# Counts and transposes moved, and a store cut in four, in a two-block transformer with three expert stages

## The chip, the cores and the metric

The kernel runs as one launch on one core of a Trainium2 chip. The engines of a core work through queues of their own: TensorE (PE, matmuls, with PEld for its weight loads), VectorE (DVE), ScalarE (ACT), GpSimd (POOL) and SyncE (SP, which here only issues transfers). The metric is the device time of one execution in microseconds; lower is better.

## The reference, cut to what matters

512 tokens of width 1024 go through two blocks, in float32.

```python
# block 1
y   = sigmoid(gate_dn) * (gated_delta_rule(q, k, v, g, beta) @ w_dn_out) \
    + sigmoid(gate_sgu) * (spatial_gating(uv) @ w_sgu_out)
h   = layer_norm(ALPHA * x + y @ w_out)
x   = layer_norm(ALPHA * h + hierarchical_moe(h))          # experts, first stage
# block 2, twice: mixer is fox attention, then mla attention
mod = silu(c) @ w_ada[i] + b_ada[i]                         # shifts, scales, gates
x   = x + g1 * mixer(rmsnorm(x) * (1 + sc1) + sh1)
x   = x + g2 * hier_moe(rmsnorm(x) * (1 + sc2) + sh2)       # experts, second and third stage
```

`hierarchical_moe` picks for each token one of 4 groups and in it 2 of 4 experts, and sums the two experts' outputs `(silu(t @ w_gate) * (t @ w_up)) @ w_down` with their weights; an expert's inner width is 256. The delta rule needs, for each of 8 heads and 8 chunks of 64 tokens, the inverse of a unit lower triangular matrix:

```python
a_mat = where(strict, (k_beta @ k.T) * decay, 0) + eye(64)
u, w  = solve(a_mat, v_beta), solve(a_mat, k_beta * exp(g_cum))
```

## The kernel before, in words

The code is one class. Most weights come as 1 MB tiles `st` on SyncE's queue (L276) and are split into a high and a low part, `wh` by ScalarE (L227) and `wl` by GpSimd or VectorE (L222); a product is then three matmuls, `x,wh`, `xl,wh` and `x,wl` (L389, L390, L391). Each engine issues in program order as the tile scheduler left it, and a tile's buffer must come free before the next tile of its ring is written. SyncE's queue is in order too: it carries the weight tiles, the stores of `ysgu` (L634) and the loads `ast` of the modulation matrix `w_ada` (L1614, three buffers), of which VectorE adds one at a time (L1626, L1628). Those additions are woven into the whole of block 1, one at each weight.

**Mixer of block 1.** `inverse(N)` is a generator. It turns 32x32 blocks of all 64 matrices at once (`T`), solves for the blocks' inverses `W` on VectorE (L907, L909) and yields; then `sgu_out` runs, eight tiles of products whose results VectorE combines with `L633` and SyncE stores (L634) from a ring of three "sy" tiles; then the generator goes on: it clears `X` and `Y` (L913, L914, 128x4096 each, GpSimd) and writes the blocks and their transposes into the diagonals (L917, L918, eight transposes on VectorE). `X` is the buffer that held the low part of sgu's gated input, so it comes free with the last sgu product. `join` then builds the 128x128 inverses from the blocks in eight steps: three cleared "q" tiles (L926) take blocks of `N` in turn (L936, GpSimd), TensorE multiplies them with X (L938) and with Y (L941, L942), ScalarE moves the product between (L940), VectorE subtracts the results from X and Y (L945). Projections for the heads are woven between the steps. The scan over chunks follows.

**Output projection of block 1.** After each of four token tiles `after(t)` normalises the rows, copies them in two pieces to `hp` on ScalarE (L507) and stores these to `hd` in DRAM on ScalarE's queue (L509). ScalarE also copies transposed tiles `xT` for the router's logits (L100), which TensorE reads (L109).

**Expert stages** (`moe`, three times). `route` turns logits into one-hot choices, positions and the row numbers of each expert's tokens (`rows`, L1195). GpSimd then fetches the rows of experts 0, 1 and 2 from `hd` with indirect transfers into `xe` (L1199). The first expert is done from unsplit weights: its rows are transposed on TensorE (`first_in`, L1223), and the gate product runs as L1236. The later experts' rows are transposed and split by `expert_in` (L1211, with `xeh` on ScalarE and `xel` on VectorE) and multiplied by L389 to L391. `behind(a, b)` makes instructions issue after the named ones. `between` is a hook that `expert_up` calls inside an expert to put the previous expert's transposes there.

## Time and profile before

| | us |
|---|---|
| three runs | 2038.22, 2036.07, 2028.91 |
| their median | 2036.07 |
| the profiled execution | 2028.85 |
| its span, first to last instruction | 2027.1 |
| TensorE busy in it | 1799.7 (89%) |

The profiled execution is one of its own, near the fastest of the runs. All rows below are from it, and times in them count from the start of its span. The mean granted TensorE clock over the span was 0.949 of full speed. In a timeline row `x3` after the shapes means that three like instructions stand in one row with their common length, and what follows in brackets is the engine's idle time before them with what ended it.

### The profile page before, as it was taken

The page shows a single profiled execution, that of the slowest core. Times are in us where ns is not written, and L with a number is a line of the kernel's source. Part 1 is how long each engine was busy: PE and PEld are TensorE (multiplying, and loading weights), DVE is VectorE, ACT ScalarE, POOL GpSimd, SP SyncE. Part 2 cuts the span into 40 slices and gives each one's busy share as a digit, 9 for nine tenths or more (in the row PEclk, how much of TensorE's full clock was granted, in tenths as well). Part 3 has the DMA queues.
Part 4 walks back from the last instruction along what each step waited for, and adds up shares of the span by engine and source line. Part 5 has one row for each costly group of instructions (what it writes and reads, how often), then busy time and mean ns, then how long its engine had stood idle before and what let it go on. Part 6 is the DMA issues. An engine that isn't in the chain of part 4 may idle for free. (4 is left out here: it accounts for less than half of the span.)

```text
span 2027.1 us, 30666 instructions
## 1 busy us (share of the span) xinstructions
PE 1799.7 (89%) x11690; PEld 1539.8 (76%) x11690; DVE 1437.6 (71%) x2580; ACT 905.8 (45%) x1706; POOL 522.8 (26%) x402
## 2 busy tenths in 40 slices
PE   6989988798989975999689999959997899996998
PEld 5778766677768775888578998958886777795886
DVE  2786885767875466677857566567988778656997
ACT  3334311223333223687334546326654366633663
POOL 5332335223334421221410001231214100242221
PEclk9999999899989987999899999979998899997999
DMA  8653455353546563798504111539973410336994
GB/s 235 190 174 118 155 175 199 99 171 104 146 124 209 200 256 121 284 360 322 173 21 125 43 64 53 219 130 338 366 285 103 127 44 22 105 156 242 364 373 173
DMA packets 174731, 363.35 MB, mean 179 GB/s; under 512 B 23086, under 2 KB 114814, under 8 KB 162288
## 3 DMA queue, kind: packets, MB, share of 16 engines
q1 hardware_dynamic: 154544, 317.94, 46.4%
q0 software_dynamic: 16528, 32.83, 4.7%
q10 hardware_dynamic: 3504, 10.54, 1.3%
q8 instruction: 94, 1.54, 0.3%
q14 instruction: 61, 0.50, 0.1%
HBM read 337.45 MB, written 47.25 MB: 190 GB/s over the span
## 5 line engine op out<-in xcount | busy, mean ns | idle before, releaser
L227 ACT ACTIVATE wh<-st 128x1024 fp32r<-128x1024 f32 (+2 forms) x331 | 360.2, 1096 | 324.1 <-PE mm L390 86.3
L222 DVE TENSOR_TENSOR wl<-st,wh 128x1024 fp32r<-128x1024 f32 (+3 forms) x250 | 319.8, 1290 | 54.6 <-ACT wh L227 51.3
L222 POOL TENSOR_TENSOR wl<-st,wh 128x1024 fp32r<-128x1024 f32 (+1 forms) x81 | 206.9, 2559 | 295.3 <-ACT wh L227 244.0
L389 PE MATMUL mm<-wh,xeh 128*128 128x256 f32 x720 | 211.4, 294 | 0.0
L390 PE MATMUL mm<-wl,xeh 128*128 128x256 f32 x720 | 204.2, 284 | 0.0
L391 PE MATMUL mm<-wh,xel 128*128 128x256 f32 x720 | 204.0, 283 | 0.0
L389 PE MATMUL mm<-x,wh 128*128 128x512 f32 x448 | 184.4, 412 | 14.8 <-DVE sy L633 12.2
L1628 DVE SCALAR_TENSOR_TENSOR acc<-ast,ca,acc 128x1024 f32<-128x1024 f32 x84 | 146.8, 1747 | 59.9 <-DMA ast<-in_w_ada_dram 58.8
L391 PE MATMUL mm<-x,wl 128*128 128x512 f32 x448 | 183.4, 409 | 0.0
L390 PE MATMUL mm<-x,wh 128*128 128x512 f32 x448 | 182.4, 407 | 0.0
L390 PEld LDWEIGHTS mm<-wl,xeh 128*128 128x128 f32 x720 | 138.6, 192 | 0.2
L389 PEld LDWEIGHTS mm<-wh,xeh 128*128 128x128 f32 x720 | 138.3, 192 | 0.2
L391 PEld LDWEIGHTS mm<-wh,xel 128*128 128x128 f32 x720 | 138.3, 192 | 0.0
L1285 POOL DMA_INDIRECT yd<-ye,rows x42 | 43.0, 1023 | 306.1 <-DVE ye L1282 193.4
L389 PEld LDWEIGHTS mm<-x,wh 128*128 128x128 f32 x448 | 87.2, 195 | 37.8 <-issue 19.1
L389 PE MATMUL mm<-wh,fXH 128*128 128x256 f32 x384 | 112.8, 294 | 0.0
L391 PE MATMUL mm<-wh,fXL 128*128 128x256 f32 x384 | 108.9, 286 | 1.8 <-DVE fXL L222 1.8
L390 PE MATMUL mm<-wl,fXH 128*128 128x256 f32 x384 | 109.9, 286 | 0.0
L390 PEld LDWEIGHTS mm<-x,wh 128*128 128x128 f32 x448 | 87.2, 195 | 17.4 <-issue 1.7
L391 PEld LDWEIGHTS mm<-x,wl 128*128 128x128 f32 x448 | 87.3, 195 | 16.4
L1268 PE MATMUL down<-st,hT 128*128 128x512 f32 x192 | 91.5, 596 | 6.0 <-ACTq L1465 3.9
L1785 DVE TENSOR_REDUCE sst<-s 128x1 f32<-128x512 f32 (+3 forms) x128 | 61.7, 484 | 46.9 <-PE s L1782 46.5
(568 smaller groups left out, 4819.0 us busy)
## 6 DMA issues: line engine op xcount, KB each, us to landing
ast<-in_w_ada_dram SPq DMA_DIRECT2D x96, 512.0 KB
st<-in_w_in_dram SPq DMA_DIRECT2D x32, 1024.0 KB
st<-in_moe_w_gate_dram SPq DMA_DIRECT2D x32, 1024.0 KB
st<-in_moe_w_up_dram SPq DMA_DIRECT2D x32, 1024.0 KB
st<-in_moe_w_down_dram SPq DMA_DIRECT2D x30, 1024.0 KB
st<-in_expert_w_gate_dram SPq DMA_DIRECT2D x16, 1024.0 KB
st<-in_expert_w_up_dram SPq DMA_DIRECT2D x16, 1024.0 KB
st<-in_expert_w_down_dram SPq DMA_DIRECT2D x15, 1024.0 KB
```

Source lines behind the costliest of these rows:

```text
L222: rest = eng.tensor_tensor(l, src, f32(h), op=ALU.subtract)
L227: return self.nc.scalar.activation(out, in_, AF.Copy)
L389: mm(out, lh, rh, start=(start and i == 0), stop=False)
L390: mm(out, lh, rl, start=False, stop=False)
L391: last = mm(out, ll, rh, start=False, stop=(stop and i == n - 1))
L1268: mm(ps[i], whole, st[:, i * 512:(i + 1) * 512], start=True, stop=False)
L1285: return self.nc.gpsimd.indirect_dma_start(out=self.yd[:, :], out_offset=bass.IndirectOffsetOnAxis(ap=dst, axis=0), in_=ye, in_offset=None ...
L1628: nc.vector.scalar_tensor_tensor(acc, st, ca[:, k:k + 1], acc, op0=ALU.mult, op1=ALU.add)
L1785: nc.vector.reduce_max(st, ps[:, :n], axis=AX.X, negate=True)
```

## The change

Four edits.

1. `after(t)`: the normalised rows go to `hd` in four pieces of 256 columns with three buffers, not in two of 512 with one.
2. `inverse`: the eight transposes are made right after the solve, before the yield, into `T` and a new tile `WT`. After the yield VectorE clears X and copies the blocks into it, GpSimd clears Y and ScalarE copies into it. `join` takes its q tiles from the "sy" ring.
3. `route`: token places, counts and the number of extra tokens are issued behind the row numbers; the pair weights behind both the fetches and the row numbers.
4. `moe`: for expert 0 the call of `expert_in` for expert 1, and the fetch behind it, move into `between`, which `expert_up` now calls after the gate product of the unsplit expert.

```diff
@@ -502,11 +502,11 @@
                 logits.finish(t, mv[:, 1:2], mv[:, 0:1])
                 xt = x[:, t, :]
                 self.normalise(xt, xt, mv, gb["ln1_g"], gb["ln1_b"])
-                for i in range(2):
-                    hp = rp.tile([P, 512], F32, tag="hp", name=self.name("hp"), bufs=1)
-                    nc.scalar.activation(hp.rearrange("t (k p) -> t k p", k=KD // 2),
-                                         turned(xt)[:, i * KD // 2:(i + 1) * KD // 2, :], AF.Copy)
-                    nc.scalar.dma_start(self.hd[t * P:(t + 1) * P, i * 512:(i + 1) * 512], hp)
+                for i in range(4):
+                    hp = rp.tile([P, 256], F32, tag="hp", name=self.name("hp"), bufs=3)
+                    nc.scalar.activation(hp.rearrange("t (k p) -> t k p", k=KD // 4),
+                                         turned(xt)[:, i * KD // 4:(i + 1) * KD // 4, :], AF.Copy)
+                    nc.scalar.dma_start(self.hd[t * P:(t + 1) * P, i * 256:(i + 1) * 256], hp)
 
             self.out_proj(x, y, logits, add, after, "e1")
             return x
@@ -856,7 +856,7 @@
             next(inv)
             self.sgu_out(gT)
             X, Y = next(inv)
-            self.t2s(c2, q=3, rt=3)
+            self.t2s(c2, rt=3)
             self.join(N, X, Y)
         with ExitStack() as c2:
             self.t2s(c2, V=3, kd=2, qv1=4)
@@ -907,21 +907,27 @@
                 nc.vector.tensor_tensor(tv, T[:, j + 1:, j:j + 1].to_broadcast([P, n, w]),
                                         W[:, j:j + 1, 0:w].to_broadcast([P, n, w]), op=ALU.mult)
                 nc.vector.tensor_tensor(W[:, j + 1:, 0:w], W[:, j + 1:, 0:w], tv, op=ALU.subtract)
+
+            V = tw.tile([P, 32, 32], F32, name="WT")
+            for j in range(4):
+                sl = slice(32 * j, 32 * j + 32)
+                nc.vector.transpose(T[sl], W[sl].rearrange("p i c -> p c i"))
+                nc.vector.transpose(V[sl], W[sl])
             yield
             X = self.big("X").rearrange("p t d -> p (t d)").rearrange("p (u s) -> p u s", u=32)
             Y = self.b16.tile([P, 32, P], F32, tag="b16", name="Y")
-            nc.gpsimd.memset(X, 0.0)
+            nc.vector.memset(X, 0.0)
             nc.gpsimd.memset(Y, 0.0)
             for j in range(4):
                 sl = slice(32 * j, 32 * j + 32)
-                nc.vector.transpose(across(X[sl, :, sl]), W[sl].rearrange("p i c -> p c i"))
-                nc.vector.transpose(across(Y[sl, :, sl]), W[sl])
+                nc.vector.tensor_copy(X[sl, :, sl], across(T[sl]))
+                self.copy("a", Y[sl, :, sl], across(V[sl]))
         yield X, Y
 
     def join(self, N, X, Y):
 
         nc = self.nc
-        qs = [self.t2("q").rearrange("p (c t) -> p c t", c=4) for _ in range(3)]
+        qs = [self.t2("sy").rearrange("p (c t) -> p c t", c=4) for _ in range(3)]
         for q in qs:
             nc.gpsimd.memset(q, 0.0)
         for u in range(8):
@@ -1121,10 +1127,11 @@
                 nc.tensor.matmul(o, ohp[:, i, k], rb[:, 2 * i + k], start=False, stop=(i + k == NT))
         rows, last = self.rows_of(pool, pi, 16)
         tok = t("tok", [P, LATE, NT])
-        self.places(tok, pi[:, 32 - LATE:32])
-        nc.vector.tensor_copy(cnt, ps[:, 64:80])
-        self.rt = dict(oh=oh, pos=pos, cnt=cnt, tok=tok)
-        self.extra_count(t)
+        with self.behind(last):
+            self.places(tok, pi[:, 32 - LATE:32])
+            nc.vector.tensor_copy(cnt, ps[:, 64:80])
+            self.rt = dict(oh=oh, pos=pos, cnt=cnt, tok=tok)
+            self.extra_count(t)
         return t, rows, ohp, last
 
     def slots_of(self, out, pos):
@@ -1235,6 +1242,8 @@
                 for k in range(KD):
                     nc.tensor.matmul(ps[:, 256 * j:256 * j + 256], xT[:, k, :], st[:, k * 256:(k + 1) * 256],
                                      start=k == 0, stop=k == KD - 1)
+                if j == 0:
+                    between()
                 continue
             for i in range(2):
                 if 2 * j + i == 3:
@@ -1331,7 +1340,7 @@
             with self.behind(last):
                 while sum(not r["raw"] for r, _ in self.ready) < 4:
                     self.prepare()
-            with self.behind(self.hold):
+            with self.behind(self.hold, last):
                 self.route_weights(t, self.lg, ohp)
                 row, after = gate, prepare(self.next, lambda: wk.tile([P, D], F32, tag="ye", name=self.name("tmp"), bufs=2))
                 if gate is not None:
@@ -1345,19 +1354,26 @@
             xT = self.first_in(wk, xe[0])
             self.fetch(src[:, 3:4], xe[0])
             for e in range(17):
-                rest = []
+                rest, coming = [], []
+
+                def tokens():
+                    if e < 15:
+                        coming.append(self.expert_in(wk, xe[(e + 1) % 3]))
+                        if e + 4 < 16:
+                            self.fetch(src[:, e + 4:e + 5], xe[(e + 1) % 3])
 
                 def between():
                     if hid is not None:
                         rest.extend(self.hidden(wk, hid))
+                    else:
+                        tokens()
 
                 if e < 16:
-                    x0 = xT
+                    if e:
+                        tokens()
+                    nxt = self.expert_up(wk, xT, w("g", e), w("u", e), between)
                     if e < 15:
-                        xT = self.expert_in(wk, xe[(e + 1) % 3])
-                        if e + 4 < 16:
-                            self.fetch(src[:, e + 4:e + 5], xe[(e + 1) % 3])
-                    nxt = self.expert_up(wk, x0, w("g", e), w("u", e), between)
+                        xT = coming[0]
                 else:
                     between()
                 if e:
```

What the scheduler makes of it, at three places. Lines of the kernel after are numbered differently: its L1644, L944, L947, L951, L1218, L1230 and L1243 are L1628, L938, L941, L945, L1211, L1223 and L1236 of before.

VectorE behind the solve, from its last step on, in the kernel before (`ast` are modulation loads, `mm` the sgu product that L633 combines):

```order
L909 TENSOR_TENSOR W<-W,tmp 128x31
L1628 SCALAR_TENSOR_TENSOR acc_2468<-ast_2473,ca,acc_2468 128x1024
L1628 SCALAR_TENSOR_TENSOR acc_2468<-ast_2507,ca,acc_2468 128x1024
L1628 SCALAR_TENSOR_TENSOR acc_2468<-ast_2543,ca,acc_2468 128x1024
L1628 SCALAR_TENSOR_TENSOR acc_2468<-ast_2546,ca,acc_2468 128x1024
L1628 SCALAR_TENSOR_TENSOR acc_2468<-ast_2580,ca,acc_2468 128x1024
L633 SCALAR_TENSOR_TENSOR sy_2460<-sy_2460,mm_2509 128x512
L633 SCALAR_TENSOR_TENSOR sy_2500<-sy_2500,mm_2548 128x512
```

and in the kernel after:

```order
L909 TENSOR_TENSOR W<-W,tmp 128x31
L914 STREAM_TRANSPOSE T<-W 32x1024
L915 STREAM_TRANSPOSE WT<-W 32x1024
L914 STREAM_TRANSPOSE T<-W 32x1024
L915 STREAM_TRANSPOSE WT<-W 32x1024
L914 STREAM_TRANSPOSE T<-W 32x1024
L915 STREAM_TRANSPOSE WT<-W 32x1024
L914 STREAM_TRANSPOSE T<-W 32x1024
L915 STREAM_TRANSPOSE WT<-W 32x1024
L1644 SCALAR_TENSOR_TENSOR acc_2477<-ast_2482,ca,acc_2477 128x1024
L1644 SCALAR_TENSOR_TENSOR acc_2477<-ast_2516,ca,acc_2477 128x1024
L633 SCALAR_TENSOR_TENSOR sy_2469<-sy_2469,mm_2518 128x512
```

The eight transposes now stand between the solve and the modulation rows, and the first L633 follows two such rows where it followed five.

VectorE in front of the join and in its first step, before (`qv` are tiles of the woven projections):

```order
L917 STREAM_TRANSPOSE X_2722<-W 32x32x32 x3
L918 STREAM_TRANSPOSE Y<-W 32x32x32 x3
L917 STREAM_TRANSPOSE X_2722<-W 32x32x32
L918 STREAM_TRANSPOSE Y<-W 32x32x32
L727 SCALAR_TENSOR_TENSOR qv_468_3065<-mm_3040,cw,qv_468_3065 128x511
L727 SCALAR_TENSOR_TENSOR qv_475_3107<-mm_3082,cw,qv_475_3107 128x511
L727 SCALAR_TENSOR_TENSOR qv_468_3065<-mm_3040,cw,qv_468_3065 128x510
L727 SCALAR_TENSOR_TENSOR qv_475_3107<-mm_3082,cw,qv_475_3107 128x510
L727 SCALAR_TENSOR_TENSOR qv_468_3065<-mm_3040,cw,qv_468_3065 128x509
L727 SCALAR_TENSOR_TENSOR qv_475_3107<-mm_3082,cw,qv_475_3107 128x509
L945 TENSOR_TENSOR X_2722<-X_2722,sc_2748 128x512
L717 SCALAR_TENSOR_TENSOR qv_468_3065<-th_3070,qv_468_3065 128x512
```

and after:

```order
L919 MEMSET X_2731 128x4096
L633 SCALAR_TENSOR_TENSOR sy_2652<-sy_2652,mm_2704 128x512
L923 COPY X_2731<-T 32x32x32 x4
L1644 SCALAR_TENSOR_TENSOR acc_3039<-ast_3044,ca,acc_3039 128x1024
L727 SCALAR_TENSOR_TENSOR qv_468_3074<-mm_3049,cw,qv_468_3074 128x511
L1644 SCALAR_TENSOR_TENSOR acc_3039<-ast_3047,ca,acc_3039 128x1024
L727 SCALAR_TENSOR_TENSOR qv_468_3074<-mm_3049,cw,qv_468_3074 128x510
L951 TENSOR_TENSOR X_2731<-X_2731,sc_2757 128x512
L727 SCALAR_TENSOR_TENSOR qv_468_3074<-mm_3049,cw,qv_468_3074 128x509
L951 TENSOR_TENSOR Y<-Y,sc_2756 128x512
L1644 SCALAR_TENSOR_TENSOR acc_3039<-ast_3089,ca,acc_3039 128x1024
L963 TENSOR_TENSOR Y<-Y,sc_2775 64x4x64
```

The transposes are gone from here, X is cleared and filled by VectorE with an L633 between, and modulation rows stand among the subtractions of the first steps: five up to the third step's.

TensorE at the first product of the join (the projection `mm` is woven in, each tile 24 matmuls), before:

```order
L391 MATMUL mm_3122<-x_183,wl_3027 128x512
L389 MATMUL mm_3122<-x_192,wh_3026 128x512
L390 MATMUL mm_3122<-x_193,wh_3026 128x512
L391 MATMUL mm_3122<-x_192,wl_3027 128x512
L938 MATMUL sc_2746<-X_2722,q_2738 128x128 x4
L389 MATMUL mm_3122<-x_201,wh_3026 128x512
L390 MATMUL mm_3122<-x_202,wh_3026 128x512
```

and after:

```order
L391 MATMUL mm_3091<-x_147,wl_2689 128x512
L389 MATMUL mm_3091<-x_156,wh_2688 128x512
L390 MATMUL mm_3091<-x_157,wh_2688 128x512
L391 MATMUL mm_3091<-x_156,wl_2689 128x512
L944 MATMUL sc_2755<-X_2731,sy_2747 128x128 x4
L389 MATMUL mm_3091<-x_165,wh_2688 128x512
L390 MATMUL mm_3091<-x_166,wh_2688 128x512
```

Before, 69 matmuls of the projections mm_3040, mm_3082 and mm_3122 stand between the last sgu product and the join's first; after, 33 of mm_3049 and mm_3091.

TensorE at the start of the second expert stage (`gen` takes transposed rows of `xe`, `mm` are expert products), before:

```order
L1223 MATMUL gen_13011<-ident,xe_12853 128x128 x4
L1211 MATMUL gen_13028<-ident,xe_12855 128x128 x4
L1236 MATMUL mm_13045<-st_12130,xeT_13010 128x256 x4
L389 MATMUL mm_13090<-wh_12944,xeh_13026 128x256
L390 MATMUL mm_13090<-wl_12945,xeh_13026 128x256
L1211 MATMUL gen_13073<-ident,xe_12857 128x128 x4
L391 MATMUL mm_13090<-wh_12944,xel_13027 128x256
```

and after:

```order
L1230 MATMUL gen_13044<-ident,xe_12886 128x128 x4
L1243 MATMUL mm_13059<-st_12163,xeT_13043 128x256 x4
L1218 MATMUL gen_13074<-ident,xe_12888 128x128 x4
L389 MATMUL mm_13123<-wh_12977,xeh_13072 128x256
L390 MATMUL mm_13123<-wl_12978,xeh_13072 128x256
L1218 MATMUL gen_13106<-ident,xe_12890 128x128 x4
L391 MATMUL mm_13123<-wh_12977,xel_13073 128x256
```

Half of the first expert's gate product now stands ahead of the second expert's transposes; the split products follow these at once.

## Rows read from the trace of the kernel before

**Rows 1.** The page: busy time, share of the span, instructions.
```profile
PE 1799.7 (89%) x11690; PEld 1539.8 (76%) x11690; DVE 1437.6 (71%) x2580; ACT 905.8 (45%) x1706; POOL 522.8 (26%) x402
```

**Rows 2.** Waits of TensorE over the span: total us, times, longest us.
```profile
PE sc L938 <- POOL q L936: 14.9, 1, 14.9
...
PE gen L1211 <- DMA xe<-hd,rows: 13.5, 3, 6.2
PE mm L389 <- DVE sy L633: 12.2, 2, 7.3
...
PE log L109 <- ACT xT L100: 3.9, 4, 3.0
```

**Rows 3.** Timeline of VectorE: start, length (us), count, idle time before and releaser.
```profile
295.72 0.18 DVE L909 TENSOR_TENSOR W<-W,tmp 128x31 f32<-128x31 f32 x1
...
311.15 1.28 DVE L1628 SCALAR_TENSOR_TENSOR acc<-ast,ca,acc 128x1024 f32<-128x1024 f32 x1 [1.40 <-DMA ast<-in_w_ada_dram]
315.40 3.30 DVE L1628 SCALAR_TENSOR_TENSOR acc<-ast,ca,acc 128x1024 f32<-128x1024 f32 x1 [2.96 <-DMA ast<-in_w_ada_dram]
318.73 1.28 DVE L633 SCALAR_TENSOR_TENSOR sy<-sy,mm 128x512 f32<-128x512 f32 x2
...
347.43 5.71 DVE L1628 SCALAR_TENSOR_TENSOR acc<-ast,ca,acc 128x1024 f32<-128x1024 f32 x2 [7.11 <-DMA ast<-in_w_ada_dram]
```

**Rows 4.** The transposing lines: count, shortest/median/longest ns, first and last start.
```profile
L917 DVE STREAM_TRANSPOSE X<-W x4: 1900/1909/2106, 353.1 to 364.7; 32x1024 f32<-32x1024 f32 x4
...
L918 DVE STREAM_TRANSPOSE Y<-W x4: 1854/1890/1895, 359.0 to 366.6; 32x1024 f32<-32x1024 f32 x4
```

**Rows 5.** Timeline of GpSimd, columns as for VectorE.
```profile
315.27 5.66 POOL L222 TENSOR_TENSOR wl<-st,wh 128x1024 fp32r<-128x1024 f32 x2 [9.25 <-ACT wh L227]
...
339.37 3.52 POOL L913 MEMSET X<- 128x4096 f32 x1 [1.48 <-PE mm L390]
...
368.46 0.99 POOL L926 MEMSET q<- 128x512 f32 x2 [12.59 <-DVE Y L918]
```

**Rows 6.** Stretches: length; PE, PEld, DVE, ACT, POOL busy; clock; DMA share; GB/s.
```profile
340.00:355.00 15.00, 15.00 (x67) 12.22 (x66) 7.85 (x4) 3.73 (x5) 15.00 (x5) 1.00 0.60 208
...
370.00:375.00 5.00, 4.91 (x21) 4.59 (x21) 2.47 (x4) 2.49 (x4) 2.46 (x8) 0.52 0.00 0
```

**Rows 7.** VectorE: a small memset (timeline), copies (group: busy us, mean ns).
```profile
0.83 0.17 DVE L159 MEMSET ones<- 128x128 f32 x1 [0.83 <-PEq L2184]
...
L229 DVE COPY xeT<-gen 128x512 f32<-128x512 f32 x3 | 2.1, 689 | 1.5 <-PE gen L1223 1.5
```

**Rows 8.** Timeline of ScalarE, 748 to 781 us.
```profile
748.77 0.35 ACTq L509 DMA_DIRECT2D hd<-hp  x1
...
756.54 1.14 ACT L507 ACTIVATE hp<-xres 128x512 f32<-128x512 f32 x1 [6.99 <-DMA hd<-hp]
...
779.78 1.21 ACT L507 ACTIVATE hp<-xres 128x512 f32<-128x512 f32 x1 [2.44 <-DMA hd<-hp]
```

**Rows 9.** Timelines of ScalarE, VectorE and GpSimd, 794 to 799 us.
```profile
794.18 0.33 ACTq L509 DMA_DIRECT2D hd<-hp  x1
...
794.84 0.18 DVE L1195 TENSOR_SCALAR rows<-gen 128x32 int32<-128x32 f32 x1
...
797.23 1.26 POOL L1199 DMA_INDIRECT xe<-hd,rows  x1 [13.49 <-DVE tot L1444]
```

**Rows 10.** Timeline of TensorE at the start of the second expert stage.
```profile
1357.09 1.09 PE L1211 MATMUL gen<-ident,xe 128*128 128x128 f32 x4 [6.23 <-DMA xe<-hd,rows]
1357.97 3.53 PE L1236 MATMUL mm<-st,xeT 128*128 128x256 f32 x8
1361.03 0.58 PE L389 MATMUL mm<-wh,xeh 128*128 128x256 f32 x1
```

**Rows 11.** Timelines of ScalarE and VectorE in that stage.
```profile
1358.22 0.60 ACT L227 ACTIVATE xeh<-gen 128x512 fp32r<-128x512 f32 x1 [6.63 <-PE gen L1211]
...
1364.54 1.23 DVE L222 TENSOR_TENSOR wl<-st,wh 128x1024 fp32r<-128x1024 f32 x1 [0.73 <-ACT wh L227]
```

## The prediction

> **What bounds the kernel now.** I read the page first: TensorE is busy 89% of the span [rows 1], so what an edit is worth is the TensorE idle time that it removes. The waits of TensorE come second [rows 2], and the change touches four of them: one of 14.9 us at the first product of the join (L938), one of 7.3 us behind the gated product of the sgu stage (L633), one of 3.0 us behind a transposed tile that ScalarE copies (L100), and 13.5 us in three waits for the second expert's rows (L1211). The timelines of the engines named as releasers come third, because a releaser is only the last link: behind L938 stand eight transposes on VectorE, not GpSimd's small copies.
>
> **The solved blocks: the wait of 7.3 us.** The solve ends at 295.72 + 0.18 = 295.9 [rows 3]. Before, VectorE then took modulation rows (L1628) until 318.7, and freed the bank that TensorE wanted with the first of two L633, at 318.73 + 0.64 = 319.4 [rows 3]. After, the order shows eight transposes, two modulation rows, then that L633. A transpose takes 1.91 or 1.89 us [rows 4], eight 15.2, which ends at 311.1. A modulation row took 1.28 us and in another place 3.30 [rows 3]. So L633 ends between 311.1 + 2.6 + 0.6 = 314.3 and 311.1 + 6.6 + 0.6 = 318.3: a gain of 1.1 to 5.1 us. I take 3.5, nearer the short end, since both loads have then long been issued.
>
> **The wait of 14.9 us.** Before, the X memset began at 339.37, released by TensorE [rows 5], the transposes ran from 353.1 to 366.6 + 1.85 = 368.4 [rows 4], and the q tiles' memsets on GpSimd had stood 12.59 us behind them [rows 5]. After, 3.5 us earlier, TensorE gives X free at about 335.9. Then on VectorE, in series:
> - X memset of 128x4096. GpSimd took 3.52 us for it [rows 5]; VectorE took 0.17 us for 128x128 [rows 7], and 32 of those are 5.4. I take 4.5, the middle.
> - L633, 0.64 us. The memset waits for TensorE at the head of VectorE's queue, and this L633 behind it frees the bank of the projection's second tile: at 341.0, and TensorE comes for it at 335.9 + 24 x 0.224 = 341.3, so it does not wait (0.6 us at the memset's upper bound).
> - four copies of 32x1024. 128x512 took 0.69 us [rows 7], the lower bound; the transposes that write the same strided block took 1.91 [rows 4], the upper. I take 1.0 each, nearer the plain copy.
>
> X is ready at 335.9 + 4.5 + 0.6 + 4.0 = 345.0 (bounds 342.8 and 349.5). TensorE reaches the first join product after 24 + 9 matmuls of the projection; 67 took 15.0 us [rows 6], 0.224 each, so 7.4 us, at 343.3. It waits 1.7 us (0 to 6.2) instead of 14.9 and gains 13.2 (8.7 to 14.9). Before, 69 such matmuls stood ahead of that product; the other 36 now stand behind it and are moved, not saved. The granted clock was 0.52 in the 5 us after the long wait [rows 6], half speed, which costs 2.4 us; without the long idle I take 2.0 of it back (0 to 2.4).
>
> Y costs nothing in this sum: its memset on GpSimd (3.52 us by X's row) and four copies on ScalarE lie beside VectorE's X. ScalarE took 1.14 us for 128x512 with a turned operand [rows 8], so a 32x1024 copy costs 1.1 to 2.3; with 1.5 Y is ready at 335.9 + 3.5 + 6.0 = 345.4, and it is first read about 7 matmuls, 1.6 us, after X. At 2.3 it would be 348.6, some 2 us late. The q tiles now use the "sy" ring, so their memsets wait for ysgu stores, with weight splits (L222) queued behind them on GpSimd. The first waits for the store of the second L633, done by 322; the nearest store took 7 us [rows 8], so 329, and GpSimd has until 335.9 for a memset of 0.5 us [rows 5] and a split. So nothing here either.
>
> **Pieces of hp.** The second piece waited 6.99 us for the store of the first, issued at 748.77, and the copy TensorE needed stood behind it [rows 8]. TensorE had then waited 3.0 us [rows 2]. With four pieces and three buffers, the fourth piece waits for the first store. If that store again takes 7 us, only about 0.5 us is won, since the last piece is half as long; if it comes as soon as in the third token tile, where the wait was 2.44 [rows 8], all 3.0. I take 2.5, since the store is half as large. At the end of this stage rows were ready at 795.0, but the first fetch started at 797.23, about 3 us after the last store was issued at 794.18 [rows 9]: the fetch waits for the store. A fourth piece that is issued about 1 us sooner brings the fetch 1.0 us forward (0 to 1.5).
>
> **Counts behind rows.** Some small VectorE instructions leave the chain to the rows. As the last store ends that chain, not the rows [rows 9], I cost this at 0. Covered so, it stays 0; uncovered, it is a few instructions like the 0.18 us one [rows 9], under 1 us.
>
> **Second expert's transposes.** Before, TensorE waited for the second expert's rows with the first's gate product behind it: 6.2 us in the second stage, and (13.5 - 6.2) / 2 = 3.65 on average in the others [rows 2]. After, part of that product runs in the wait. By the order that is the first half of the gate product, four matmuls that the trace records as eight, 3.53 us [rows 10]. It fits into each wait. What follows the transposes is then limited by their evacuation: the rows land at 1357.09, ScalarE's xeh ends at 1358.22 + 0.60 = 1358.8 [rows 11], and the first split product can start there instead of at 1361.03 [rows 10]: 2.2 us. Some of the following products will run at half clock, as those before them did, so I take 1.5 in each stage (0 to 3.5). In the second stage a copy also moves ahead of a split of 1.23 us [rows 11]; I add 1.0. Together 5.5 (0 to 11). The fetch for expert 4 moves along on GpSimd; its rows are read three experts later.
>
> **Sum.** 3.5 + 13.2 + 2.0 + 2.5 + 1.0 + 5.5 = 27.7 us; all low bounds give 1.1 + 8.7 + 0 + 0.5 + 0 + 0 = 10.3, all high ones 5.1 + 14.9 + 2.4 + 3.0 + 1.5 + 11 = 37.9. The profiled execution took 2028.85 us, so it would take 2001.2. The median of the three runs, 2036.07, lies 7.2 above it, at the upper end of 2028.91 to 2038.22; against the median the sum is 2008.4. I predict 2008, own range 1998 to 2026.
>
> **Rivals.**
> - *The transposes delay L633.* If a modulation load also arrives late, by the 2.96 us of [rows 3], L633 ends at 318.3 + 3.0 = 321.3, 1.9 us later than before instead of 3.5 earlier: 5.4 less, 2014. For it: 15 us of new work ahead of it. Against: five modulation rows stood there before, and two are left. 0.10.
> - *Copies and GpSimd shut each other out.* A modulation row took 3.30 us from 315.40 and 1.28 from 311.15 [rows 3]; GpSimd's splits ran from 315.27 for 5.66 us [rows 5]: 2.0 more beside them. Four copies and the memset, each 2.0 later, make X 10 us later; the stall is 11.7 and the clock falls again: 12 less, 2020. Against: GpSimd's Y memset should be over when the copies start. 0.08. (The Trainium skill, SBUF — State Buffer, section Who interferes with whom, says that an fp32 copy within SBUF takes a pair of ports that VectorE shares with GpSimd, and that whoever comes second is blocked for a whole instruction. The 3.30 us row agrees with such blocking for a two-input instruction; no row shows it for a copy. By that rule this rival, not the sum, would hold.)
> - *The gain is given back.* Join and scan behind it are a chain; if the scan waits for loads that start when they did, the 18.7 us of the first three terms go: 9 left, 2027. Against: loads are issued as buffers come free, so they move along. 0.10.
> - *Not what it says.* Counts behind rows gain nothing, as costed; if the expert stages gain nothing either, since the rows' landing sets their end anyway, 22.2 are left, 2014. For it: cold products. Against: the 2.2 us that L389 started after its operand. 0.04.
> - *Slower.* In the join VectorE's order now puts five modulation rows between the first subtractions that TensorE waits for. The longest wait for such a load was 7.11 us, and two rows behind it took 5.71, 2.85 each [rows 3]. Five times 7.11 + 2.85 is 49.8; less 27.7 that is 22 us slower, 2058. It makes the change a loss from three such waits on, and one above 0.5% from four. For it: the new order. Against: SyncE issues those loads before the join starts. 0.06.
>
> **Chances.** The forecast 0.62. A difference below 0.5%, about 10 us, can't be told from none in this kernel. Faster by more: the forecast, the first two rivals and the fourth, but for 0.02 in their low corner: 0.82; within: the gain given back and that corner, 0.12; slower: 0.06. The range, 1994 to 2027, leaves out half of the given-back case and the slower one; below it reaches 4 us past the own range, since the profiled execution itself lies 7 us under the median.
>
> **What would show it.** Right: the first L633 after the solve ends at 314 to 318 us; the wait of the first join product is under 6 us, with no half clock behind it; no wait of 3 us at L109; the first split product of each expert stage starts within 2 us of the rows' landing. Wrong: a wait of TensorE on X's copies or memset above 6 us, waits in the join on a subtraction that stands behind L1628 on VectorE, or scan waits longer than before.

## The result, and the profile after

The changed kernel takes **2019.57 us** (median of 11 runs, 2009.97 to 2030.86), the kernel before 2036.07 (11 runs beside it, 2027.93 to 2041.52): a ratio of **0.9926, 95% interval 0.9905 to 0.9947**. The forecast was 2008, with a range of 1994 to 2027. The profiled executions stand 2027.1 against 2011.9 us of span, 15.2 us apart, where the sum said 27.7.

The page of the kernel after, the same rows as [rows 1]:

```profile
span 2011.9 us, 30690 instructions
PE 1808.3 (90%) x11690; PEld 1546.0 (77%) x11690; DVE 1439.5 (72%) x2585; ACT 914.4 (45%) x1718; POOL 518.8 (26%) x401
```

To see where the 15.2 us came from, I took the same matmul in both traces at some landmarks, each with as many matmuls ahead of it in both, and subtracted its start after from its start before. A difference between two landmarks is what the stretch between them gained.

| landmark | start before | start after | ahead by | gain of the stretch | the sum had |
|---|---|---|---|---|---|
| ahead of the sgu wait (L391) | 301.39 | 300.90 | 0.49 | | |
| sgu product behind it (L389) | 335.17 | 328.12 | 7.05 | 6.6 | 3.5 |
| behind join and scan (L391) | 607.14 | 599.73 | 7.41 | 0.4 | 15.2 |
| router's product (L109) | 758.54 | 750.27 | 8.27 | 0.9 | 2.5 |
| first expert's first product (L1223, now L1230) | 803.61 | 794.39 | 9.22 | 0.95 | 1.0 |
| second stage, routing (L1099, now L1105) | 1340.52 | 1329.39 | 11.13 | 1.9 | 1.5 |
| third stage, router (L109) | 1822.08 | 1809.02 | 13.06 | 1.9 | 2.5 |
| third stage, a later expert's transposes (L1211, now L1218) | 1865.64 | 1852.47 | 13.17 | 0.1 | 1.5 |

One term of the sum failed: join and scan, 0.4 instead of 15.2. (Read at the scan's last transposes, L883, the kernel is 9.17 us ahead and the stretch seems to gain 2.1; but five projection matmuls that stood ahead of these transposes now stand behind them. The expectations of runs 1 and 9 still count up to there.) The other terms came out within 3.1 us of theirs; the last 2.0 of the 15.2 us stand behind the last landmark. The waits of TensorE between 300 and 375 us say how; the last column is the idle time ahead of a group and what ended it, and they answer to [rows 2]:

```profile
L391 PE MATMUL mm<-gh,wl 128*128 128x512 f32 x24 | 10.2, 426 | 2.8 <-POOL wl L222 2.8
L389 PE MATMUL mm<-gh,wh 128*128 128x512 f32 x23 | 9.8, 427 | 0.7 <-DVE sy L633 0.7
L944 PE MATMUL sc<-X,sy 128*128 128x128 f32 x30 | 5.6, 334 | 7.2 <-DVE X L923 7.2
L947 PE MATMUL sc<-rt,Y 128*128 128x128 f32 x24 | 4.8, 363 | 3.5 <-DVE Y L963 3.5
```

The wait at the sgu stage fell from 7.3 to 0.7. The first join product (L938, now L944) still waits 7.2, for a copy of X, and the third join step has at L947 a wait of 3.5 that did not exist, for the last subtraction of the second step. VectorE in that stretch, which answers to [rows 3, 4] (start, duration, then the idle time before it and its releaser):

```profile
307.95 4.62 DVE L1644 SCALAR_TENSOR_TENSOR acc<-ast,ca,acc 128x1024 f32<-128x1024 f32 x2
312.61 0.69 DVE L633 SCALAR_TENSOR_TENSOR sy<-sy,mm 128x512 f32<-128x512 f32 x1
...
334.10 3.47 DVE L919 MEMSET X<- 128x4096 f32 x1 [0.80 <-issue]
337.60 0.69 DVE L633 SCALAR_TENSOR_TENSOR sy<-sy,mm 128x512 f32<-128x512 f32 x1
338.21 8.92 DVE L923 COPY X<-T 32x1024 f32<-32x1024 f32 x4
...
366.34 1.28 DVE L1644 SCALAR_TENSOR_TENSOR acc<-ast,ca,acc 128x1024 f32<-128x1024 f32 x1 [5.21 <-DMA ast<-in_w_ada_dram]
367.54 0.41 DVE L963 TENSOR_TENSOR Y<-Y,sc 64x256 f32<-64x256 f32 x1
```

And GpSimd beside it, which answers to [rows 5]:

```profile
335.11 0.53 POOL L932 MEMSET sy<- 128x512 f32 x1 [5.01 <-DMA ysgu<-sy]
335.70 0.61 POOL L942 COPY sy<-N 32x128 f32<-32x128 f32 x2
336.28 1.00 POOL L1640 DMA_DIRECT2D row<-in_b_ada_dram  x2
337.32 3.51 POOL L920 MEMSET Y<- 128x4096 f32 x1
340.92 2.90 POOL L222 TENSOR_TENSOR wl<-st,wh 128x1024 fp32r<-128x1024 f32 x1
343.93 1.36 POOL L932 MEMSET sy<- 128x512 f32 x1
```

Read the two side by side. The four copies of X took 3.39, 3.21, 1.25 and 1.03 us one by one. The first ends 0.77 us after GpSimd's clearing of Y (340.83), the second 1.00 us after its weight split (343.82); the last two, beside shorter GpSimd rows, are near the 1.0 of the sum. GpSimd's rows are stretched too: the small clearing took 1.36 instead of 0.53. Y was being cleared then because the q tile's clearing ahead of it on GpSimd's queue had waited 5.01 us for a ysgu store.

Windows of all engines show what the two waits cost beyond themselves (busy time, granted clock in the column PEclk); they answer to [rows 6]:

```profile
340.00:347.00 7.00, 0.00 (x0) 0.00 (x0) 6.96 (x4) 6.10 (x4) 6.70 (x5) 0.72 0.33 129
347.00:352.00 5.00, 4.82 (x15) 4.19 (x16) 3.77 (x5) 4.01 (x4) 2.16 (x4) 0.50 0.35 107
355.00:360.00 5.00, 5.00 (x45) 4.42 (x44) 4.24 (x7) 1.61 (x3) 0.71 (x2) 1.00 0.57 165
368.00:373.00 5.00, 4.91 (x21) 4.29 (x22) 3.15 (x5) 0.00 (x0) 0.00 (x0) 0.50 0.34 107
```

TensorE ran at 0.50 (1.2 GHz) in the 5 us behind each, where the kernel before had one such stretch, behind its single wait [rows 6]. Each costs at least 2.5 us: the half clock lasted from 347.2 to 353.3 and from 368.1 to 373.8, before from 370.1 to 374.8. That is 11.8 us against 4.7, so by the half some 3.5 us more.

The rest of the profile: the fourth piece of hp waited for the store of the first, which answers to [rows 8]. Issued at 740.71, that store let go of its buffer at 748.76.

```profile
748.76 0.67 ACT L507 ACTIVATE hp<-xres 128x256 f32<-128x256 f32 x1 [6.13 <-DMA hd<-hp]
749.84 0.66 ACT L100 ACTIVATE xT<-gen 128x256 f32<-128x256 f32 x2 [0.40 <-ACT hp L507]
```

Of TensorE's waits for fetched rows over the span, those for the second expert (L1211, now L1218), 13.5 us in [rows 2], are nearly gone. Those for the first expert (L1223, now L1230) were 11.9 of 22.1 us of waiting there and are 18.0 of 23.9.

```profile
PE gen L1230 <- DMA xe<-hd,rows: 18.0, 2, 9.0
...
PE gen L1218 <- DMA xe<-hd,rows: 0.8, 1, 0.8
```

### The profile page after: what moved, and what is told of

Read it like the earlier page. It is cut to its first block, busy times and chain, and to the rows that moved or that the text cites. A ratio compares the mean times of both kernels' runs of the same rounds, so it can differ in the third digit from the quotient of the medians.

```text
span 2011.9 us, 30690 instructions
## 1 busy us (share of the span) xinstructions
PE 1808.3 (90%) x11690; PEld 1546.0 (77%) x11690; DVE 1439.5 (72%) x2585; ACT 914.4 (45%) x1718; POOL 518.8 (26%) x401
## 5 line engine op out<-in xcount | busy, mean ns | idle before, releaser
L222 DVE TENSOR_TENSOR wl<-st,wh 128x1024 fp32r<-128x1024 f32 (+3 forms) x250 | 319.7, 1290 | 51.0 <-ACT wh L227 47.1
L222 POOL TENSOR_TENSOR wl<-st,wh 128x1024 fp32r<-128x1024 f32 (+1 forms) x81 | 207.3, 2563 | 304.1 <-ACT wh L227 260.1
L389 PE MATMUL mm<-wh,xeh 128*128 128x256 f32 x720 | 210.8, 293 | 2.1 <-ACT xeh L227 2.1
L391 PE MATMUL mm<-wh,xel 128*128 128x256 f32 x720 | 204.2, 284 | 0.0
L389 PE MATMUL mm<-x,wh 128*128 128x512 f32 x448 | 185.2, 413 | 7.5 <-DVE sy L633 4.9
L391 PE MATMUL mm<-x,wl 128*128 128x512 f32 x448 | 182.1, 406 | 0.0
L1644 DVE SCALAR_TENSOR_TENSOR acc<-ast,ca,acc 128x1024 f32<-128x1024 f32 x84 | 142.5, 1696 | 52.6 <-DMA ast<-in_w_ada_dram 51.5
L389 PEld LDWEIGHTS mm<-wh,xeh 128*128 128x128 f32 x720 | 137.8, 191 | 3.1 <-ACT xeh L227 3.0
L391 PEld LDWEIGHTS mm<-wh,xel 128*128 128x128 f32 x720 | 137.9, 192 | 0.0
L391 PE MATMUL mm<-wh,fXL 128*128 128x256 f32 x384 | 110.3, 289 | 4.6 <-DVE fXL L222 4.6
L389 PE MATMUL mm<-wh,fXH 128*128 128x256 f32 x384 | 113.7, 296 | 0.6 <-ACT fXH L227 0.6
L389 PEld LDWEIGHTS mm<-x,wh 128*128 128x128 f32 x448 | 87.0, 194 | 29.7 <-issue 11.9
L391 PEld LDWEIGHTS mm<-x,wl 128*128 128x128 f32 x448 | 86.5, 193 | 17.5 <-issue 0.9
```

The source lines that it names most:

```text
L222: rest = eng.tensor_tensor(l, src, f32(h), op=ALU.subtract)
L389: mm(out, lh, rh, start=(start and i == 0), stop=False)
L391: last = mm(out, ll, rh, start=False, stop=(stop and i == n - 1))
L1644: nc.vector.scalar_tensor_tensor(acc, st, ca[:, k:k + 1], acc, op0=ALU.mult, op1=ALU.add)
```

## The experiments

My theory after the result: VectorE's copies are held by GpSimd's rows, and GpSimd's rows are where they are because the q tiles use the ring sy. The rival: the copies are slow by themselves, and the gain was lost in the scan.

**1. The early transposes alone** (before, with the inverse and the join of after):

```
-            self.t2s(c2, q=3, rt=3)
+            self.t2s(c2, rt=3)
...
+                nc.vector.transpose(T[sl], W[sl].rearrange("p i c -> p c i"))
+                nc.vector.transpose(V[sl], W[sl])
...
-                nc.vector.transpose(across(X[sl, :, sl]), W[sl].rearrange("p i c -> p c i"))
+                nc.vector.tensor_copy(X[sl, :, sl], across(T[sl]))
```

> The kernel before with the edit of inverse and join alone. Read off the two traces at like instructions, this edit gave 6.4 us up to the end of the sgu products and about 2 us more up to the end of the scan. If the edits add up: 7 to 9 us faster than before, ratio 0.9955 to 0.9965, with a wait of 7 us at the first join product. If the gain of the whole came from the other three edits and the join's was noise between two executions: within 3 us of before.

Measured 2024.78 us, ratio 0.9961 (0.9945 to 0.9977). The sgu stretch gained 6.5 us, join and scan 2.3. The same edit in the same place, alone, gives the same poor return at the join, so no other part of the change spoils it. Here Y's clearing was all but over as the copies began: the first took 1.16 us, and only the second, beside GpSimd's split, 3.14. The first join product still waited 4.9 us, and the third step 4.8 behind a modulation row that waited 6.54 for its load.

**2. All the rest** (after, with the inverse and join of before):

```
+            nc.gpsimd.memset(X, 0.0)
+                nc.vector.transpose(across(X[sl, :, sl]), W[sl].rearrange("p i c -> p c i"))
...
-        qs = [self.t2("sy").rearrange("p (c t) -> p c t", c=4) for _ in range(3)]
+        qs = [self.t2("q").rearrange("p (c t) -> p c t", c=4) for _ in range(3)]
```

> The changed kernel with inverse and join as they were before: pieces of hp, counts behind rows and the second expert's transposes remain. Read off the traces they gave 0.8 us at the pieces, 0.9 at the first fetch, 2.6, 3.3 and 0.1 us at the three expert stages: 7 us, ratio about 0.9965. If fetches only happened to land otherwise in that one execution: 2 to 4 us, 0.998 to 0.999.

Measured 2027.99 us, ratio 0.9978 (0.9951 to 1.0005), so by the ratio alone it can't be told from no change, nor can the two expectations be told apart. In its profile the wait of the first join product is back at 14.90 us. Join and scan, whose code here is that of before, came out 3.0 us shorter all the same: a single execution strays that much, so the 0.4 us of the changed kernel is no measured gain. The two halves, 0.39% and 0.22%, are 0.61% together, which the interval of the whole (0.53% to 0.95%) holds.

**3. The q tiles in a ring of their own** (after, with one line of before):

```
-            self.t2s(c2, rt=3)
+            self.t2s(c2, q=3, rt=3)
...
-        qs = [self.t2("sy").rearrange("p (c t) -> p c t", c=4) for _ in range(3)]
+        qs = [self.t2("q").rearrange("p (c t) -> p c t", c=4) for _ in range(3)]
```

> The changed kernel with a ring of their own for the q tiles, so that GpSimd waits for no ysgu store and clears Y some 4 us sooner. Theory (GpSimd's instructions block VectorE's copies into X): the first copy no longer takes 3.4 us and the second 3.2; the four together fall from 8.9 to about 5 to 6 us, and the wait at the first join product from 7.2 to 3 to 5 us, 2 to 4 us faster than the changed kernel. Rival (the copies are slow because they read at a stride): 8.9 us and 7.2 us stay.

Measured 2009.46 us, ratio 0.9891 (0.9858 to 0.9924); span 2005.2, 6.7 below the changed kernel's. VectorE and then GpSimd in its timeline:

```profile
337.63 5.51 DVE L923 COPY X<-T 32x1024 f32<-32x1024 f32 x4
...
332.90 3.52 POOL L920 MEMSET Y<- 128x4096 f32 x1 [0.43 <-PE mm L391]
336.39 2.40 POOL L222 TENSOR_TENSOR wl<-st,wh 128x1024 fp32r<-128x1024 f32 x1
343.19 1.45 POOL L932 MEMSET q<- 128x512 f32 x3 [4.41 <-DVE X L923]
```

Y is cleared 4.4 us earlier, the split ends at 338.8, and only the first copy meets it: 2.13 us, then 1.13, 1.17 and 1.04. The first join product waits 2.92 us, the 3.5 us wait behind it is gone, and join and scan gained 12.7 us (ahead by 6.70 at the L389 landmark, 19.37 behind the scan): most of the 15.2 us that the sum had. That is more than the 2 to 4 us expected, as the second wait and its half clock went too. What is left of the wait is the q tiles' own clearing, 4.41 us behind X's copies, presumably since the new ring takes the memory of the tiles that those copies read.

**4. The stride moved from the copies to the transposes** (after, with):

```
-                nc.vector.transpose(T[sl], W[sl].rearrange("p i c -> p c i"))
-                nc.vector.transpose(V[sl], W[sl])
+                nc.vector.transpose(across(T[sl]), W[sl].rearrange("p i c -> p c i"))
+                nc.vector.transpose(across(V[sl]), W[sl])
...
-                nc.vector.tensor_copy(X[sl, :, sl], across(T[sl]))
+                nc.vector.tensor_copy(X[sl, :, sl], T[sl])
```

> The changed kernel with the stride moved from the copies to the early transposes: these write at a stride, and the copies into X and Y read in order. Rival (stride): the four copies into X fall from 8.9 to about 4.5 us, those into Y from 8.0 to about 4.5, the wait from 7.2 to about 3. Theory (GpSimd blocks): the first two copies into X still end no sooner than GpSimd's memset of Y and its next weight split, some 6 us after the first copy starts; the four take 7.5 to 8.5 us and the wait stays at 6 to 7. The transposes take 2 to 3 us more, hidden or added to the sgu wait, in both.

Measured 2018.28 us, ratio 0.9932 (0.9902 to 0.9961).

```profile
343.27 7.13 DVE L923 COPY X<-T 32x1024 f32<-32x1024 f32 x4
351.11 1.28 DVE L1644 SCALAR_TENSOR_TENSOR acc<-ast,ca,acc 128x1024 f32<-128x1024 f32 x1 [0.72 <-DMA ast<-in_w_ada_dram]
```

The copies that nothing held took 0.68 and 0.69 us, the two beside GpSimd's clearing and split still 2.98 and 2.73. So the stride costs about 0.35 us a copy and the blocking about 2.2. The first join product waited 4.50 us, between what the two theories gave, and the third step 5.56 at L947, behind a modulation row that waited 7.29 for its load. That is the rival "slow by themselves" answered: the first two are slow with either form, and only there.

**5. The pieces of hp on GpSimd** (after, with):

```
-                    nc.scalar.activation(hp.rearrange("t (k p) -> t k p", k=KD // 4),
-                                         turned(xt)[:, i * KD // 4:(i + 1) * KD // 4, :], AF.Copy)
-                    nc.scalar.dma_start(self.hd[t * P:(t + 1) * P, i * 256:(i + 1) * 256], hp)
+                    nc.gpsimd.tensor_copy(hp.rearrange("t (k p) -> t k p", k=KD // 4),
+                                          turned(xt)[:, i * KD // 4:(i + 1) * KD // 4, :])
+                    nc.gpsimd.dma_start(self.hd[t * P:(t + 1) * P, i * 256:(i + 1) * 256], hp)
```

> The changed kernel, with the rows of the first expert layer's input copied and stored by GpSimd and its queue instead of by ScalarE. The changed kernel's fourth copy of a block stood 6.13 us on ScalarE behind the first store, and the product after it waited 2.35 us for ScalarE's copy of x. Theory one, that wait on the engine is what is left of the stall there: with the copies off ScalarE the product's wait of 2.35 us is gone or under 0.8, and the time is about 2 us below that of the changed kernel (0.1%, less than the interval of a ratio; the rows decide). Theory two, the store is the bound and not the engine that stands behind it: the wait of that product goes, and the first fetch of the expert layer, which reads those rows, starts later by about as much, so that the first product of the expert layer waits 9 us and more and the end is where it was.

Measured 2015.74 us, ratio 0.9898 (0.986 to 0.9936), which can't be told from the changed kernel's. The product's waits by group:

```profile
L109 PE MATMUL log<-wr,xT 128*128 128x20 f32 x192 | 25.5, 250 | 0.9 <-ACT xT L100 0.7
```

In the changed kernel this idle time was 3.3 us. So the engine queue was the wait, as theory one has it. But three waits ahead of the first expert grew, at L1105 to 5.86 us from 5.48, at L1125 to 2.40 from 1.36 and at L1230 to 9.22 from 9.00. From the start of this layer to the router's product the stretch gained 2.5 us more than in the changed kernel, and up to the first expert's product only 0.5 more: theory two, mostly.

**6. No modulation row among the first four join steps' subtractions** (after, with):

```
-        for _ in range(2 if self.slots_left % 5 == 0 else 1):
-            next(self.ada, None)
+        with self.behind(getattr(self, "joined", None)):
+            for _ in range(2 if self.slots_left % 5 == 0 else 1):
+                next(self.ada, None)
...
+            if u == 3:
+                self.joined = done
```

> The changed kernel, with the modulation rows that are taken after the join's definition put behind the join's fourth step on VectorE, so that none stands between the first four steps' subtractions. In the changed kernel one of them waited 5.21 us for its weights, and the product of the second join step after it waited 3.48 us for the subtraction behind it. Theory one, the row that waited for its load cost these 3.48 us: that wait falls under 1 us, the first join product's wait of 7.21 us stays within 1 us, and the profiled span is about 3 us shorter. Theory two, the subtraction was late on account of the Y half (ScalarE's four copies of 8.03 us in all, of which the last ends at 348.9) and the row only filled the time: the wait stays at 2.5 to 3.5 us and the span as well.

Measured 2013.12 us, ratio 0.9887 (0.985 to 0.9924). TensorE's groups from 340 to 375 us:

```profile
L945 PE MATMUL sc<-X,sy 128*128 128x128 f32 x40 | 7.2, 323 | 4.8 <-DVE X L924 4.8
L948 PE MATMUL sc<-rt,Y 128*128 128x128 f32 x35 | 4.9, 280 | 0.0
```

The 3.5 us wait is gone (one of 1.9, for a subtraction from X, came in the first step), and from 353 us on the clock is 1.00 where the changed kernel fell again. ScalarE's copies of Y end at 350.0 here, no earlier in relation to X, so it was the row that waited for its load: theory one. That load stood on SyncE's queue behind a weight tile that had waited 4.9 us for a GpSimd split. The first wait is 4.8 instead of 7.2; X's clearing began 1.6 us before Y's instead of 3.2, so less of the copies met GpSimd's rows. Join and scan gained 7.7 us. The span, 2016.8, is longer than the changed kernel's all the same: this execution was 3.7 us later ahead of the sgu wait, and lost 6.0 us between 1243 and 1268 us of the kernel before (the changed kernel 0.3), where its clock was 0.51 from 1237 to 1251 us of its own time, in code that the edit doesn't touch. Such spells come and go from one execution to the next, so the stretch and the median bear the verdict.

**7. The counts ahead of the rows again** (after, without `with self.behind(last):` around them, and with `self.behind(self.hold)` as before).

> The changed kernel with the counts put back ahead of the rows, all else as changed. In the third expert stage of every kernel that has the counts behind the rows the second fetch took 3.4 us on GpSimd, and in those without it 2.0. Theory one, the four weight splits of VectorE that now fall beside the fetches make them longer: with the counts back the second fetch of that stage takes 2.0 us again, the second expert's rows land some 1.3 us sooner, and the third stage gains 1 to 1.5 us on the changed kernel, the rest being equal. Theory two, the fetch's time follows from something else in that stage (the queue's load or the new order of the second expert's tokens): it stays at 3.4 us, and the stage gains nothing or loses up to 0.5 us, as the counts take their place again ahead of the fetch.

Measured 2014.97 us, ratio 0.9912 (0.9883 to 0.9941). GpSimd's fetches in the third stage, of the changed kernel first, then of this one:

```profile
1820.39 3.37 POOL L1206 DMA_INDIRECT xe<-hd,rows  x1 [0.30 <-issue]
1824.06 1.67 POOL L1206 DMA_INDIRECT xe<-hd,rows  x1 [0.30 <-issue]
```

```profile
1823.52 2.02 POOL L1205 DMA_INDIRECT xe<-hd,rows  x1 [0.30 <-issue]
1825.85 0.99 POOL L1205 DMA_INDIRECT xe<-hd,rows  x1 [0.30 <-issue]
```

That is what theory one said, 2.02 and a stage that gains 2.4 us where the changed kernel's gained 0.1. But runs 5 and 6 and 8 have the counts behind the rows too, and there the same fetch took 1.01 and the next one 2.02. The following rows are of run 5:

```profile
1824.24 1.01 POOL L1206 DMA_INDIRECT xe<-hd,rows  x1 [0.30 <-issue]
1825.55 2.02 POOL L1206 DMA_INDIRECT xe<-hd,rows  x1 [0.30 <-issue]
```

So my generalisation falls: the time goes not with the counts, but with where VectorE's weight splits (L222, 1.22 us each, nearly back to back) stand to the fetch. In the changed kernel the fetch began 0.025 us ahead of a split's start and lasted over two splits; in run 5 it began 0.029 us ahead of one and took 1.01. In the kernel before and in this run it began 0.07 us into a split, and ended 0.88 us after that split's end. The stage's fourth fetch, some 10 us later, took 1.05 in every kernel. The counts' small VectorE rows, of 0.19 us and less, now lie between other splits and shift them.

**8. Y cleared by VectorE** (after, with):

```
-            nc.gpsimd.memset(Y, 0.0)
+            nc.vector.memset(Y, 0.0)
```

> The changed kernel with the clearing of Y on VectorE instead of GpSimd. In the changed kernel the first two of the four copies that build X took 3.39 and 3.21 us, ending where GpSimd's clearing of Y and its weight split end, and the last two 1.25 and 1.03. Theory one, VectorE's copy and GpSimd's work shut each other out: GpSimd's weight split now lies earlier, VectorE clears Y in about 3.5 us ahead of the copies, each of the four copies takes 1.0 to 1.3 us unless a GpSimd row lies right beside it, X is ready at about 346 and the first join product waits 6 to 7 us, no less than before the edit by more than 1 us. Theory two, the first copies are slow by themselves (their strided source, or the wait for the clearing of X): the first two take 3 us and more again, X is ready at about 350 and the product waits 10 us and more.

Measured 2010.99 us, ratio 0.9885 (0.9852 to 0.9919). VectorE, then GpSimd:

```profile
340.96 3.47 DVE L920 MEMSET Y<- 128x4096 f32 x1 [0.80 <-issue]
344.35 6.54 DVE L923 COPY X<-T 32x1024 f32<-32x1024 f32 x4
...
340.79 6.76 POOL L222 TENSOR_TENSOR wl<-st,wh 128x1024 fp32r<-128x1024 f32 x1 [1.42 <-ACT wh L227]
```

This time the work is on the other engine, and GpSimd's split took 6.76 us instead of 2.39, over the whole of VectorE's clearing and into the copies. What held it is open: X's clearing on VectorE, just as long, stood from 335.96 to 339.43 beside a split that took 2.39. Of the copies, the first two lay beside that long split and took 0.98 and 3.46, the others 1.03 and 1.03. So theory one holds for the copies, not for its times. X was ready at 350.9, the figure of theory two, for another reason (the split that theory one had put earlier), and the product waited 4.8 us, below both, since TensorE came to it 6 us later.

**9. Put together**: run 3's ring, run 4's stride for X alone, run 7's counts.

> The version that the runs so far point to: the changed kernel with the ring of q of its own again, with X's transposes writing the order that X's copies read (T without a stride, as in the third of the runs), and with the counts back ahead of the rows. By the profiles so far its parts give, against the kernel before: the sgu part 6.4 us, join to scan's end 14 us (the run with the ring of q of its own), the expert layer's input 2 us, the three expert stages 2.6, 3 and 2.3 us, and some 3 us of loss to drift between them: about 26 us, so some 2007 us where the kernel before has 2033 (ratio 0.987). Theory one, the causes are independent and add up: ratio 0.984 to 0.989, the first join product waits under 3 us, no modulation row waits 5 us for a load between the first four join steps. Theory two, what is freed at the join is given back where the same loads and the same GpSimd rows come due, as in the changed kernel: ratio 0.991 to 0.994, with a wait of 3 us and more at the second or third join step.

(Where this text has "the third of the runs" for the stride, run 4 is meant.)

Measured 2011.97 us, ratio 0.9894 (0.9872 to 0.9915), between the two theories' bounds and no better than run 3. Rows of its timeline, VectorE's copies and GpSimd's second fetch of the third stage:

```profile
338.62 3.23 DVE L923 COPY X<-T 32x1024 f32<-32x1024 f32 x4
...
1809.03 3.16 POOL L1205 DMA_INDIRECT xe<-hd,rows  x1 [0.31 <-issue]
```

TensorE's groups over its span:

```profile
L944 PE MATMUL sc<-X,q 128*128 128x128 f32 x64 | 10.1, 293 | 1.3 <-POOL q L942 1.3
L947 PE MATMUL sc<-rt,Y 128*128 128x128 f32 x64 | 8.6, 278 | 1.3 <-ACT rt L946 1.3
L958 PE MATMUL sc<-X,N 64*64 64x64 f32 x64 | 5.4, 224 | 2.4 <-DVE X L951 2.4
```

The copies are short, 3.23 us for all four. Join and scan gained 12.8 us, as in run 3: three short waits took the place of one of 2.92. And the counts are ahead of the rows, yet the third stage's second fetch took 3.16 us, which is the second refutation of theory one of run 7. It began 0.07 us into a split, as in run 7, where it took 2.02: the start beside a split doesn't decide it alone either. Runs 3, 6, 8 and 9 lie at 0.9885 to 0.9894, with intervals that overlap each other's and, by a little, the changed kernel's (0.9905 upwards): that they beat it is likely, not settled. All beat the kernel before.

## Why the prediction was right, and where its sum was off

**Right**: faster by more than 0.5% and within the range, but not by the largest step named. The sum was 12.5 us too large; the join's step fell short by 14.8, and the sgu step made up 3.1 of that. Two of the prediction's own signs of being wrong came up, a wait on X's copies above 6 us (7.2) and one on a subtraction behind L1628 (3.5). That the time fell within the range all the same is owed to the other terms and to the range's width: for the join it was luck.

**The sgu wait, 3.5: measured 6.6.** The mechanism held, and the gain lies above the term's high bound of 5.1. The transposes were cheaper than [rows 4] made them: VectorE's first L633 started at 312.61 and ended at 313.3, ahead of the 314 to 318 of the sign, and of the eight transposes ahead of it four took 2.03 us and four, which read without a stride, 1.19; the sum had 1.9 for all.

**The join's first product, 13.2, and the clock, 2.0: measured 0.4 for both, scan included** (2.3, -0.5 and 2.5 in runs 1, 5 and 7, which have the same join). The failed step reads: "GpSimd's Y memset should be over when the copies start". It began at 337.32. The step on the sy ring weighed the first q tile's clearing alone, with 329 as the end of its wait; that one began at 324.2. The second q tile's clearing, also ahead of Y's in GpSimd's queue, waited for the store of the third L633, issued at 326.56, until 335.1. So the rival "copies and GpSimd shut each other out", to which 0.08 was given, is what happened: four copies took 8.92 us, not 4.0 (X's clearing, at 3.47 instead of 4.5, gave 1.0 back). Run 3 shows the cause by moving GpSimd's rows away, run 4 by taking the stride out, and runs 1 and 8 by which copies were held. (The Trainium skill, SBUF — State Buffer, section Who interferes with whom, says that whichever of the two engines gets the shared ports first holds them for a whole instruction while the other stands. The trace agrees: 3.39 and 3.21 us for copies that take 0.98 to 1.17 where nothing of GpSimd's holds them.) Besides, TensorE reached the product at 339.97, not 343.3, so more of X's time lay open. Then the "slower" rival came true once: a modulation row waited 5.21 us for its load, ahead of a subtraction, and cost 3.48 (run 6). Together: 14.9 - 7.2 = 7.7 won, less 3.5, less some 3.5 for more time at half clock, is 0.7; measured 0.4, which a single execution's straying would hide anyway. Y's copies, costed at nothing beside X, took 8.03 us instead of 6.0 and ended at 348.9; no wait of TensorE on them shows, X being late too. The "given back in the scan" rival did not happen: with the join mended in run 3, 12.7 us came through behind the scan.

**Pieces of hp, 2.5: measured 0.75** (from 7.60 just ahead of the first block's wait to 8.35 at the routing). A size, near the low bound of the term: the first store of half the size kept its buffer for 8.1 us from its issue, against 7.8 for the whole one before (748.77 to 756.54). "I take 2.5, since the store is half as large" was the wrong end. **Earlier fetch, 1.0: 0.9.**

**Expert stages, 1.5, 2.5, 1.5.** Read over each stage's own products: 2.6, 3.25 and 0.1 (ahead by 9.22 and then 11.8, 11.13 and 14.39, 13.06 and 13.17), in sum 6.0 against 5.5. The mechanism held: the waits for the second expert's rows fell from 13.5 to 0.8 us. The third stage's gain was eaten by the late second fetch, which the step "I cost this at 0" did not see: it counted the counts' time, not what they move.

Between landmarks some 1 to 3 us, and 6 in run 6, are lost or won from one execution to the next that no edit explains, in part in spells of half clock; I leave them open. Open too is what decides the race of fetch and split within 0.005 us.

## What to carry to other kernels

When an operation moves to an engine to be quick, look at what its neighbour does in those same microseconds, and at what the neighbour's queue waits for: here a shared tile ring delayed a clearing by 4.4 us, and the copies it then met were the critical path. A row queued between two that TensorE waits for must have its load landed. And a store of half the size need not be done sooner: here it took 8.1 us instead of 7.8.

## What the runs showed of the hardware

- A VectorE copy of 32x1024 fp32 took 0.98 to 1.17 us where nothing of GpSimd's held it and up to 3.46 beside a GpSimd clearing or split. A GpSimd split took 2.39 alone, 2.39 beside one VectorE clearing, and in one place 6.76 beside another clearing and the copy behind it.
- A fetch by row indices on GpSimd took 1.05 us with no VectorE split beside it, and 2.0, 3.2 or 3.4 beside VectorE's two-operand splits. With a lead of 0.023 to 0.027 us over a split's start it took 3.4 in four kernels, with one of 0.029 to 0.032 it took 1.0 in three.
- A stride on the reading side made a VectorE transpose 2.03 instead of 1.19 us (one on the writing side about as much, 1.96 to 2.08 in run 4), ScalarE's copy 2.0 instead of 1.05, and VectorE's copy 1.03 instead of 0.68.
- VectorE cleared 128x4096 in 3.47 us, GpSimd in 3.51.
